# Column halves in two PSUM banks, four block places per parity, one output store: a masked prefix sum with a product, on one core

## The chip, the core and the metric

The kernel runs on one core of one Trainium2 chip. The metric is the device time of one execution in microseconds (us). Each figure is the median of several executions. A "span" is one execution as the hardware profiler recorded it; it is some 2 us shorter than the timed figure of the same execution (86.72 beside 88.84). An execution is called slow when it lies over 1.5% above the fastest of the same kernel; fast is compared with fast.

## The reference

```python
B, S, D = 8, 8192, 512
mask = pos < lengths                      # lengths: 8 numbers between 16 and 8191
cs = np.cumsum(x * mask, axis=1)          # x: [8, 8192, 512] float32
mid_features = cs[b, lengths[b] // 2]     # one row of 512 numbers per batch row
out = mid_features @ w                    # w: [512, 512]; out: [8, 512]
```

Only one element of the prefix sum is used, so a batch row needs the plain sum of its first n = min(length, length // 2 + 1) positions. For this draw n is 570, 2690, 256, 2057, 905, 3772, 3859 and 571. Nothing else of x is read: 31.2 MB with the weights.

## The kernel before

A batch row is cut into whole blocks of 512 positions (a `[128, 4, 512]` tile, 1 MB) and a remainder below 512. The first block of row 0 has a buffer of its own. That leaves 1, 5, 0, 4, 1, 7, 7 and 1 whole blocks for rows 0 to 7. SyncE (SP) issues the blocks, ScalarE (ACT) the remainders, TensorE adds everything up in one PSUM bank: the weights are a 128 x 8 selector with ones in the row's column, and the four position groups j of a block go to four column groups of the array (`tile_position`), so four matmuls run side by side (in the trace the eight records of a block, 0.77 us each in the mean, fit into 1.04 to 1.90 us). Rows of even and odd number ("parity" q) have separate buffers.

```python
NB = S // 2 // BLK                                   # 8
xt = sb("xt", [P, 2, NB, G, D])                      # 8 places per parity
s_ps = ps("s_ps", [P, D])                            # one bank, 512 columns
...
# SyncE, for each row; base, n from the lengths
def load_block(k):
    take(sp, s_free[q][k], 1)                        # wait for the place, count down
    sp.dma_start(out=xt[:, q, k], in_=...).then_inc(s_full[q][k], 16)
...
# TensorE, for each row: remainder first, then its blocks
take(pe, s_rem[q], 16 * (len(PARTS) + 1))
for j in range(G):
    mm = add(j, cur[:, q, B + j * B:2 * B + j * B], rem[:, q, j])
mm.then_inc(s_rfree[q], 1)
def add_block(k):
    take(pe, s_full[q][k], 16)
    for j in range(G):
        mm = add(j, cur[:, q, :B], xt[:, q, k, j])   # 128x512 each
    mm.then_inc(s_free[q][k], 1)                     # the place is free again
whole_blocks(pe, ns.rows(q), add_block)
...
# the end: VectorE copies sums (two halves), TensorE folds, VectorE copies,
# TensorE multiplies by wt, then
for j in range(2):   # VectorE; ScalarE does j = 2, 3 into o_sb[1]
    step(dve.tensor_copy, out=o_sb[0][:, j * P:(j + 1) * P], in_=o_ps[32 * j:32 * j + B, :P])
sp.dma_start(out=out[:, :D // 2], in_=o_sb[0][:]).then_inc(s_out, 16)
act.dma_start(out=out[:, D // 2:], in_=o_sb[1][:]).then_inc(s_out, 16)
```

The row loop is a hardware loop over pairs of rows; the block count of a row is known only from the lengths, in registers (`whole_blocks` nests comparisons). Each row starts again at place 0.

## Time and profile before

| | before |
|---|---|
| timed, median (4 fast runs) | 88.96 us (88.77 to 89.65) |
| profiled span | 86.72 us |
| first block issued by SP | 5.07 us |
| last block of x landed | 79.08 us |
| from there to the end of the span | 7.64 us |
| TensorE busy | 49.5 us (57%) |
| transfers, mean over the span | 361 GB/s (some 420 while they run) |

The table reads as three stretches: a start of some 4 us until data flow, a middle in which the transfer engines set the pace, and a tail in series after the last landing.

### The profile page before, as it was taken

To read this page: it belongs to the slowest core of one execution; us is meant where nothing else is said; L and a number is where in the kernel's file an instruction comes from. 1 tells how busy PE (TensorE), PEld (TensorE's weight loads), DVE (VectorE), ACT (ScalarE), POOL (GpSimd) and SP (SyncE) were. 2 spreads that over 40 slices of the span, in tenths; PEclk is the share of its full clock that TensorE was granted. 3 is DMA by queue.
4 is the path that set the end of the run, shared out by engine and by line. 5 is a ranking of instruction groups with operands and counts; after the bars stand their busy time and mean duration, and the time that the engine had idled before them with its cause. 6 is when DMAs were issued, how large, how long until landed. Compare 5 with 4: busy or idle time off the path is not lost. (4 is left out here: it accounts for less than half of the span.)

```text
span 86.7 us, 1276 instructions
## 1 busy us (share of the span) xinstructions
PE 49.5 (57%) x317; PEld 9.1 (10%) x317; DVE 8.1 (9%) x42; ACT 2.0 (2%) x4; POOL 4.0 (5%) x9
## 2 busy tenths in 40 slices
PE   0910533999367627179833268877933348779720
PEld 0400000022011000012100000001100000011710
DVE  3685000000000000000000000000000000000520
ACT  0000000000000000000005100000000000000020
POOL 0980000000000000000000000000000000000000
PEclk9999999999999996557998555555999985559995
DMA  2799999999999999999999999999999999980000
GB/s 30 325 412 283 397 417 420 430 427 419 419 408 416 416 423 423 401 416 423 423 423 419 416 428 423 423 423 408 423 423 423 423 419 419 423 359 15 0 4 3
DMA packets 4693, 31.28 MB, mean 361 GB/s; under 512 B 658, under 2 KB 674, under 8 KB 946
## 3 DMA queue, kind: packets, MB, share of 16 engines
q1 hardware_dynamic: 3762, 27.27, 76.5%
q10 hardware_dynamic: 928, 3.97, 11.7%
q8 instruction: 1, 0.02, 0.1%
q14 instruction: 2, 0.02, 0.0%
HBM read 31.23 MB, written 0.02 MB: 360 GB/s over the span
## 5 line engine op out<-in xcount | busy, mean ns | idle before, releaser
L339 PE MATMUL s_ps<-xt,cur 128*8 128x512 f32 x200 | 34.0, 771 | 21.9 <-PEq L103 21.8
L339 PE MATMUL s_ps<-rem,cur 128*8 128x512 f32 x64 | 10.5, 738 | 3.6 <-PEq L103 3.6
L339 PEld LDWEIGHTS s_ps<-xt,cur 128*8 128x8 f32 x200 | 4.3, 91 | 50.5 <-issue 50.4
L322 DVE COPY cur<-table 128x40 f32<-128x40 f32 x8 | 1.4, 184 | 53.0 <-PE s_ps L339 53.0
L339 PE MATMUL s_ps<-first,first_w 128*8 128x512 f32 x8 | 1.9, 1040 | 5.1 <-DMA first<-in_x_dram 5.1
L257 POOL MEMSET rem<- 128x2048 f32 x2 | 3.5, 1804 | 0.0
L347 PE MATMUL s_ps<-zero 1*128 1x512 f32 x2 | 2.1, 1131 | 2.4 <-DVE n_i L268 2.4
L339 PEld LDWEIGHTS s_ps<-rem,cur 128*8 128x8 f32 x64 | 1.6, 93 | 13.1 <-issue 13.0
L268 DVE COPY s_sb<-s_ps 128x256 f32<-128x256 f32 x2 | 0.8, 425 | 18.4 <-PE s_ps L376 18.4
L240 ACT ACT_TABLE_LOAD x1 | 1.3, 1283 | 46.5 <-issue 46.5
L382 PE MATMUL mf_ps<-fold,s_sb 128*128 128x8 f32 x8 | 1.1, 260 | 0.5 <-DVE s_sb L268 0.5
L243 ACT COPY o_sb<-o_ps 8x128 f32<-8x128 f32 x2 | 0.5, 260 | 35.0 <-PE o_ps L390 35.0
L390 PE MATMUL o_ps<-wt,mf_sb 128*8 128x128 f32 x32 | 1.1, 273 | 0.0
L382 PEld LDWEIGHTS mf_ps<-fold,s_sb 128*128 128x128 f32 x8 | 1.0, 190 | 0.6 <-DVE s_sb L268 0.6
L350 PEld LDWEIGHTS n_ps<-n_f,ones 1*128 1x128 f32 x2 | 0.7, 332 | 1.0 <-DVE table L268 0.5
L390 PEld LDWEIGHTS o_ps<-wt,mf_sb 128*8 128x8 f32 x32 | 0.8, 89 | 0.0
L347 PEld LDWEIGHTS s_ps<-zero 1*128 1x128 f32 x2 | 0.5, 304 | 2.3 <-DVE n_i L268 2.3
L339 PEld LDWEIGHTS s_ps<-first,first_w 128*8 128x8 f32 x8 | 0.2, 90 | 5.1 <-issue 5.1
L268 DVE COPY o_sb<-o_ps 8x128 f32<-8x128 f32 x2 | 0.6, 280 | 0.9 <-PE o_ps L390 0.8
L268 DVE MEMSET zero<- 1x512 f32 x1 | 0.5, 485 | 1.1 <-SPq L48 1.1
L268 DVE TENSOR_SCALAR thr_i<-thr_i 128x2 int32<-128x2 int32 x1 | 0.5, 484 | 0.0
L350 PE MATMUL n_ps<-n_f,ones 1*128 1x8 f32 x2 | 0.4, 286 | 0.0
(36 smaller groups left out, 5.5 us busy)
## 6 DMA issues: line engine op xcount, KB each, us to landing
xt<-in_x_dram SPq DMA_DIRECT2D x25, 1024.0 KB, 14.4
rem<-in_x_dram ACTq DMA_DIRECT2D x3, 512.0 KB, 7.1
wt<-in_w_dram ACTq DMA_DIRECT2D x1, 1024.0 KB, 6.8
first<-in_x_dram SPq DMA_DIRECT2D x1, 1024.0 KB, 8.2
rem<-in_x_dram ACTq DMA_DIRECT2D x3, 256.0 KB, 6.5
rem<-in_x_dram ACTq DMA_DIRECT2D x3, 128.0 KB, 6.6
rem<-in_x_dram ACTq DMA_DIRECT2D x3, 32.0 KB, 5.8
rem<-in_x_dram ACTq DMA_DIRECT2D x1, 64.0 KB, 6.1
```

Of the source, the lines that this page charges most:

```text
L240: act.copy(out=warm[:], in_=zero[:, :1])
L243: copy = act.copy(out=o_sb[1][:, j * P:(j + 1) * P], in_=o_ps[64 + 32 * j:64 + 32 * j + B, :P])
L257: pool.memset(rem[:, q], 0.0).then_inc(s_rfree[q], 1)
L268: do(*args, **kw).then_inc(s_dve, 1)
L322: dve.tensor_copy(out=cur[:, b % 2], in_=table[:, b * WT:(b + 1) * WT]).then_inc(s_cur[b % 2], 1)
L339: return pe.matmul(s_ps[32 * j:32 * j + B], lhsT=weights, rhs=rows, start=False, stop=False, skip_group_check=True, tile_position=(0, 32 * j))
L347: pe.matmul(s_ps[:], lhsT=zero[:, :P], rhs=zero[:], start=True, stop=False, skip_group_check=True)
L350: pe.matmul(n_ps[:, :B], lhsT=ones[:], rhs=n_f[:], start=True, stop=True).then_inc(s_pe, 1)
L382: mm = pe.matmul(mf_ps[h][:, i * B:(i + 1) * B], lhsT=s_sb[:, 2 * h + i], rhs=fold[:], start=True, stop=True)
L390: mm = pe.matmul(o_ps[32 * j:32 * j + B, :P], lhsT=mf_sb[:, kc], rhs=wt[:, kc, j * P:(j + 1) * P], start=(kc == 0), stop=(kc == KC - 1), t ...
```

## The change

The intent: let the first half of the columns finish early, so that its copy and its fold lie beside the second half's matmuls (two PSUM banks, a chained counter `s_half`); let all four output quarters be one copy and one store; let SyncE load only the lengths of two rows at a time, so that it issues its first block earlier; and halve the buffers of the blocks: eight places of 1 MB per parity become four.

```diff
+    NP = 4
-    xt = sb("xt", [P, 2, NB, G, D])
+    xt = sb("xt", [P, 2, NP, G, D])
-    s_ps = ps("s_ps", [P, D])
+    s_ps = [ps(f"s_ps{h}", [P, D]) for h in range(2)]
-    mf_sb = sb("mf_sb", [P, KC, B])
-    o_sb = [sb(f"o_sb{h}", [B, D // 2]) for h in range(2)]
+    mf_sb = sb("mf_sb", [P, KC, 32])
+    o_sb = sb("o_sb", [P, P])
-    ctx.enter_context(tc.tile_critical(no_gpsimd_drain=True))
+    ctx.enter_context(tc.tile_critical(sync_engine=mybir.EngineType.Pool, no_gpsimd_drain=True))
@@ SyncE
-        ns = Counts(sp, s_len1, 16)
+        ns = Counts(sp, s_len1, 16, loaded=2)     # next_pair() loads the next 4 words
-                    take(sp, s_free[q][k], 1)
-                    sp.dma_start(out=xt[:, q, k], ...).then_inc(s_full[q][k], 16)
+                    take(sp, s_free[q][k % NP], 1)
+                    sp.dma_start(out=xt[:, q, k % NP], ...).then_inc(s_full[q][k % NP], 16)
-        sp.dma_start(out=out[:, :D // 2], in_=o_sb[0][:]).then_inc(s_out, 16)
+        sp.dma_start(out=out.rearrange("b (j c) -> j b c", c=P), in_=o_sb[::4]).then_inc(s_out, 16)
@@ ScalarE: its two copies, its activation table and its store are gone
@@ VectorE
+        dve.wait_ge(s_half, due)                  # due: blocks + remainders, from the lengths
         for h in range(2):
+            if h:
+                dve.wait_ge(s_pe, B + 2)
-            step(dve.tensor_copy, out=s_sb[:, 2 * h:2 * h + 2], in_=cols[:, 2 * h:2 * h + 2])
+            step(dve.tensor_copy, out=s_sb[:, 2 * h:2 * h + 2], in_=s_ps[h][:, :H]...)
-        for j in range(2):
-            step(dve.tensor_copy, out=o_sb[0][:, ...], in_=o_ps[32 * j:32 * j + B, :P])
+        step(dve.tensor_copy, out=o_sb[:], in_=o_ps[:, :P])
@@ TensorE
+            for h in range(2):
+                for j in range(G):
+                    mm = pe.matmul(s_ps[h][32 * j:32 * j + B, :H], lhsT=weights[j],
+                                   rhs=rows[:, j, h * H:(h + 1) * H], ...)
+                mm.then_inc((half, done)[h], 1)
-                        whole_blocks(pe, ns.rows(q), add_block)
+                    with pe.Fori(0, NB // NP):
+                        whole_blocks(pe, n, NP, add_block)
+                        pe.reg_alu(n, n, NP * BLK, ALU.subtract)
+                        pe.reg_alu(n, n, 0, ALU.max)
```

Cut: the matching changes of counts and semaphores, the column order of the weights, and the split of TensorE's program into two branches (`sums()`, `product()`).

## The prediction

> **What bounds the kernel now.** I read the page's slices first, then the groups of instructions, the DMA issues, the waits of the load queue, and last the chain and the end of the timeline. In the slices the transfers run full from slice 2 to slice 35 of 40, and nothing else does:
>
> ```profile
> PE   0910533999367627179833268877933348779720
> DMA  2799999999999999999999999999999999980000
> GB/s 30 325 412 283 397 417 420 430 427 419 419 408 416 416 423 423 401 416 423 423 423 419 416 428 423 423 423 408 423 423 423 423 419 419 423 359 15 0 4 3
> ```
>
> A slice is 86.7/40 = 2.17 us. From about 4 us to 78 us the 16 transfer engines move some 420 GB/s; the one hole is slice 3 (283). So the middle costs bytes over rate: a block of 128 x 4 x 512 floats is 1.05 MB, 2.49 us. TensorE only follows:
>
> ```profile
> L339 PE MATMUL s_ps<-xt,cur 128*8 128x512 f32 x200 | 34.0, 771 | 21.9 <-PEq L103 21.8
> ```
>
> It stood idle 21.9 us ahead of the block sums, nearly all of it in line 103, the taking of a "full" semaphore. A cheaper TensorE, fewer matmuls or fewer waits there buy nothing in the middle; what can move the time is (a) a hole in the transfers, and (b) what comes before the first and after the last transfer. The end, in the timeline:
>
> ```profile
> 79.21 1.04 PE L339 MATMUL s_ps<-xt,cur 128*8 128x512 f32 x8
> 80.19 0.17 PE L376 MATMUL s_ps<-zb 1*32 1x1 bf16 x1
> 80.40 0.88 DVE L268 COPY s_sb<-s_ps 128x256 f32<-128x256 f32 x2 [18.36 <-PE s_ps L376]
> 80.88 1.07 PE L382 MATMUL mf_ps<-fold,s_sb 128*128 128x8 f32 x8 [0.52 <-DVE s_sb L268]
> 81.88 1.06 PE L390 MATMUL o_ps<-wt,mf_sb 128*8 128x128 f32 x32
> 83.00 0.59 DVE L268 COPY o_sb<-o_ps 8x128 f32<-8x128 f32 x2 [0.84 <-PE o_ps L390]
> 83.56 0.58 ACTq L246 DMA_DIRECT2D out_dram<-o_sb  x1
> 83.63 0.36 SPq L191 DMA_DIRECT2D out_dram<-o_sb  x1
> ```
>
> The last block lands at 79.1; then 7.6 us in series: sums, copy, fold, copy, product, copy, store, closing handshake. How far ahead the loads are issued is in the issues and in the load queue's own waits:
>
> ```profile
> xt<-in_x_dram SPq DMA_DIRECT2D x25, 1024.0 KB, 14.4
> ...
> SPq L103 <- SPq L103: 21.6, 8, 9.2
> ```
>
> A block lands 14.4 us (median) after its issue, so about six blocks' worth of bytes (14.4/2.49) stand queued. The queue's own 21.6 us of waiting for free places does no harm only because of that depth.
>
> **What the Trainium skill says.** (1) "PSUM — Partial Sum Buffer", Terms: TensorE writing and VectorE reading the same bank and quadrant at once is an error. So a copy of half the sums beside the other half's matmuls needs two banks, as the change has. The trace agrees in so far as the copy begins only after the closing matmul (80.19, then 80.40). (2) "DMA: Bandwidth & Descriptors", Anatomy of one DMA: a fixed cost of about 2.0 us per transfer besides its bytes (stated for the GpSimd path). This trace, on the hardware queues: the weights' transfer was issued at 0.92, and the stretch 0 to 2.8 us moved 47 GB/s on average, the next 0.4 us 328; so data come about 2 us after the issue on an idle queue. (3) Same page, "Why a DMA increments its semaphore by 16 and not by 1": the engine count is the largest up to 16 that divides both sides' slowest dimension. The new store has slowest dimensions 32 and 4, so by that it would use 4 engines; no run yet shows it. (4) "TensorE: Matmul & The Clock Gate", Part 1: the clock is at half or full, set by recent activity. The trace has both: a block's eight matmul records take 1.04 us at full clock and 1.89 at half.
>
> **The change part by part.**
>
> Four places instead of eight per parity. The lengths of this draw give rows of 570, 2690, 256, 2057, 905, 3772, 3859 and 571 summed positions, so whole blocks 1, 5, 0, 4, 1, 7, 7, 1 (the first one of row 0 has its own buffer). Rows 1, 3, 5, 7 share parity 1. Block k of a row goes to place k modulo 4, and each row begins at place 0 again. Before, row 1 fills places 0 to 4, and row 3's block 0 waits for row 1's block 0. After, row 1's block 4 goes to place 0, and row 3's block 0 needs that same place: it can be issued only when row 1's *last* block is summed. Row 2 has no block. So at that moment no block is in flight at all, and SP issues in order, so nothing behind it can go out either. This is the step that I expect to decide.
>
> Size of that hole. Before, row 1's block 4 was issued at 8.87 and landed 15.6 later, at 24.5. After, its issue waits for row 1's block 0, summed at about 20.0 (SP's next issue, into that place, is at 20.24). Its data then come from 22 on; row 2's remainder (512 KB, issued 16.89) fills most of that gap, so it lands at about 24.4 still. Then: 0.15 to the first matmul, 1.04 for the sums, 0.05 for the semaphore (25.65); 0.22 for SP to take it and issue (20.01 to 20.24 in this trace); 2.0 until data: 27.9. A packet of 8 KB takes 0.31 at full flow, so flow is back at 27.6. The transfer engines ran dry not at 24.4 but spread over the 1.2 us before (first to last engine's landing of one block), on average 23.8. Loss 27.6 - 23.8 = **3.8 us**. Only the 32 KB remainder of row 3 can fill it: row 4's is issued after row 2's remainder is summed (27.19 now). Since every later byte queues behind, the whole loss goes to the end.
>
> Other places where four bind: rows 5 and 6 (7 blocks). Block 4 of a row waits for its block 0, with blocks 1 to 3 in flight: 3 x 2.49 = 7.5 us against some 4.0 for sum, issue and latency (1.9 + 0.2 + 2.0, half clock). Row 7's block 0 needs a place that row 5 freed long ago. No hole: 0.
>
> Two banks, sums by column halves. A block is 16 records of 256 columns in place of 8 of 512: the same columns. I take the same 0.86 to 1.04 us (1.9 at half clock), under 2.49 in any case: 0 in the middle. At the end half 0 is done about 0.43 earlier, so its copy (0.43) and its fold lie beside the matmuls of half 1. Before: copy, copy, fold, fold with the second copy and half the folds in the chain. The chain loses about one copy, 0.43; but TensorE's sequencer must leave two nested loops and a second branch before the closing matmul and the fold, which I put at 0.2. Gain **0.25**.
>
> Output: one copy of 128 x 128 for two of 8 x 128 (0.28 each, the partitions don't count): gain **0.3**. One store on SP alone instead of two; if 4 engines carry 8 pieces of 512 B each, the landing is some 0.2 later: **-0.2**. GpSimd leads the closing handshake rather than SP: after the landing SP no longer starts a round and collects it: **0.25**, an estimate from the 1.5 us between landing (85.1) and end.
>
> Lengths by pairs. SP loads 4 register words instead of 16 before its first block issue at 5.07. If half of the load's 1.2 us goes with the words, it is 0.4 earlier. That shrinks the hole at 8 us:
>
> ```profile
> 8.00:9.00 1.00, 0.00 (x0) 0.00 (x0) 0.00 (x0) 0.00 (x0) 0.00 (x0) 1.00 0.58 197
> 9.00:10.00 1.00, 0.30 (x4) 0.15 (x8) 0.00 (x0) 0.00 (x0) 0.00 (x0) 1.00 1.07 426
> ```
>
> There 0.5 us of flow is missing ((426-197)/426), and 0.2 in the us before (344). I take **0.25** of it. The later loads of pairs (four of about 0.8) lie in SP's waits: 0. The dropped activation table load (1.28 at 46.5) and the smaller clearing matmuls are beside transfers: 0.
>
> Sum: +3.8 - 0.25 - 0.3 + 0.2 - 0.25 - 0.25 = **+2.95**; I take off 0.3, because the hole might be partly filled by remainders. 88.94 + 2.65 = **91.6 us**.
>
> **The rivals.** (A) The hole isn't there or is small, because enough is queued. For it: four blocks are 10 us of transfers, and in the rows of seven this suffices. Against it: the place arithmetic above, where the last block itself holds the place. If it held, only gains of 0.85 remain: 88.1. (B) TensorE becomes the bound: 16 short matmuls with 16 weight loads (91 ns each) and two increments per block. For it: at half clock a block already takes 1.89 of 2.49. Against it: the matmuls work on four column groups side by side and the weight loads overlap. If the cost rose by a third at half clock, some 20 blocks would go to 2.5: at most +1 more. (C) The last block falls in a half-clock phase: 1.89 for 1.04 and slower products, +1.0 at the end; in the trace before it fell in a full-clock one (1.00 there). (D) The hole is wider: the sum of row 1's block 4 at half clock, +0.85, or the loop's second pass and instruction fetch on TensorE, +0.5.
>
> **Range and chances.** The hole, 3.3 to 4.5; gains, 0.4 to 1.6; C adds up to 1. That is 90.2 to 92.9 for 8 in 10. Two per cent slower is 90.72, so slower 0.75; within 2% 0.20 (a hole under 2.7, or gains at their upper end with it); faster, under 87.16, needs A and larger gains: 0.05.
>
> **What would show it.** In the slices of after: one slice near 24 to 28 us falls from 420 to under 150 GB/s, and its neighbour dips; all later slices at 420; last landing near 82. SP's longest waits for a place include one that ends just after row 1's last block is summed, and the next block's issue stands at about 25.9, not 20.2. The end from last landing to end of span takes about 7.0 us for 7.6; the first copy of sums starts before the last block's matmuls end. First block issue near 4.6. The prediction is wrong if the slices from 22 to 30 us stay at 420, if a second hole appears in rows 5 to 7, or if blocks' matmuls exceed 2.4 us.

## The result

The changed kernel took 94.31 us (median of 4 runs: 93.89, 94.09, 94.52 and 95.42, the last one slow) against 88.96. The ratio is 1.0571, 95% interval 1.0487 to 1.0654: **slower by 5.7%**, some 5.3 us. The predicted direction was right, but 91.6 and the range to 92.9 were too low. (A ratio here is the mean time of one kernel's fast runs over the mean of the other's fast runs of the same rounds, so it is not quite the ratio of the medians that I quote.)

The profiled spans differ by 5.96 us, 86.72 and 92.68. The clock of TensorE, the share and the flow of the transfers in 40 slices of 2.32 us, after:

```profile
PEclk9999999999985985555579975555589998556998
DMA  2899999966708999999999999999999999970000
GB/s 28 332 426 426 415 412 414 417 262 187 294 0 301 428 424 420 419 420 424 424 424 424 408 422 419 428 417 424 424 424 424 421 424 417 417 308 0 0 9 2
```

Slice 3 (from 7 us) is full now, where the kernel before had its dip of 283. In its place there are **two** holes: slices 8 to 10 (18.5 to 25.5 us: 262, 187, 294) and slices 11 and 12 (0 and 301). From slice 13 on the flow is as before. What the queue of the block loads and TensorE waited for, after, in that order as three views (the issue group with its median time from issue to landing; the queue's waits: us in total, times, longest; TensorE's group for block sums: busy us, mean ns of one, idle us before it and what ended most of that):

```profile
xt<-in_x_dram SPq DMA_DIRECT2D x25, 1024.0 KB, 10.8
```

```profile
SPq L109 <- SPq L109: 46.5, 12, 12.8
```

```profile
L367 PE MATMUL s_ps<-xt,cur 128*8 128x256 f32 x400 | 35.7, 495 | 22.9 <-PEq L109 22.9
```

A block is in flight 10.8 us instead of 14.4, SP waits 46.5 us for free places instead of 21.6, and TensorE's busy time on blocks grew only from 34.0 to 35.7 us. So nothing on TensorE became a bound; the loads are issued later.

The holes by the microsecond. Columns: stretch, its length, busy time of PE, PEld, DVE and POOL, granted clock, DMA share, GB/s:

```profile
20.00:21.00 1.00, 1.00 (x24) 0.49 (x20) 0.00 (x0) 0.00 (x0) 1.00 0.18 74
21.00:22.00 1.00, 1.00 (x24) 0.46 (x20) 0.00 (x0) 0.00 (x0) 1.00 0.61 107
22.00:23.00 1.00, 0.84 (x16) 0.21 (x8) 0.00 (x0) 0.00 (x0) 1.00 0.58 238
...
25.00:26.00 1.00, 0.50 (x12) 0.33 (x16) 0.00 (x0) 0.00 (x0) 1.00 0.01 4
26.00:27.00 1.00, 0.74 (x16) 0.20 (x12) 0.00 (x0) 0.00 (x0) 1.00 0.00 0
27.00:28.00 1.00, 1.00 (x16) 0.36 (x8) 0.18 (x1) 0.00 (x0) 0.52 0.19 33
28.00:29.00 1.00, 0.95 (x15) 0.18 (x11) 0.00 (x0) 0.00 (x0) 0.50 0.54 180
29.00:30.00 1.00, 1.00 (x16) 0.30 (x8) 0.18 (x1) 0.00 (x0) 0.50 1.03 434
```

The same view of the kernel before (with a column for ACT ahead of POOL) is full in both places:

```profile
20.00:21.00 1.00, 1.00 (x12) 0.21 (x8) 0.00 (x0) 0.00 (x0) 0.00 (x0) 1.00 1.06 442
...
27.00:28.00 1.00, 0.82 (x8) 0.27 (x12) 0.00 (x0) 0.00 (x0) 0.00 (x0) 1.00 1.04 434
```

The end, from the timeline of after (start, length in us, engine, what it does, how many; in brackets the idle time before it and what ended it):

```profile
82.89 1.94 PE L367 MATMUL s_ps<-rem,cur 128*8 128x256 f32 x16
84.59 1.27 PE L367 MATMUL s_ps<-xt,cur 128*8 128x256 f32 x16
85.51 0.95 DVE L281 COPY s_sb<-s_ps 128x256 f32<-128x256 f32 x2 [18.73 <-PE s_ps L367]
85.80 0.17 PE L405 MATMUL s_ps<-zb 1*32 1x1 bf16 x1
85.99 1.14 PE L412 MATMUL mf_ps<-fold,s_sb 128*128 128x8 f32 x8
87.06 1.08 PE L420 MATMUL o_ps<-wt,mf_sb 128*32 128x128 f32 x32
88.21 0.29 DVE L281 COPY o_sb<-o_ps 128x128 f32<-128x128 f32 x1 [0.86 <-PE o_ps L420]
88.52 0.73 SPq L211 DMA_DIRECT2D out_dram<-o_sb  x1
```

The mechanism that the change aims at is there: the first copy of sums begins at 85.51, before the last sums end (85.86), and the output copy is one of 0.29. But the last sums end 2.3 us after the last landing (83.57), and the store lands at 91.35, 2.83 us after its issue.

The stages of the profiled executions side by side, read from the traces (us; each stage begins where the one above it ends). "After, again" is a second profile of the unaltered changed kernel, taken with other runs; "five places" and "pairs" are experiments told below.

| | before | after | after, again | five places | pairs |
|---|---|---|---|---|---|
| first block issued at | 5.07 | 4.33 | 4.33 | 4.33 | 4.38 |
| row 1's fifth block issued / landed | 8.87 / 24.45 | 20.56 / 25.37 | 19.94 / 24.98 | 7.81 / 25.26 | - / 24.27 |
| row 3's first block issued / landed | 20.24 / 27.14 | 26.84 / 31.60 | 26.45 / 31.42 | 20.52 / 27.81 | 19.88 / 26.91 |
| last block landed at | 79.08 | 83.57 | 83.33 | 79.68 | 78.85 |
| then: its sums end | 1.18 | 2.30 | 1.18 | 1.19 | 1.18 |
| closing matmul ends | 0.10 | 0.10 | 0.70 | 0.70 | 0.10 |
| fold and product end | 2.58 | 2.17 | 3.00 | 2.14 | 2.58 |
| store issued | 0.63 | 0.39 | 0.39 | 0.39 | 0.63 |
| store landed | 1.57 | 2.83 | 2.59 | 2.62 | 1.57 |
| end of the span | 1.58 | 1.32 | 1.32 | 1.35 | 1.57 |
| span | 86.72 | 92.68 | 92.52 | 88.06 | 86.48 |

So of the 5.96 us, 4.49 stand at the last landing and 1.47 in the tail. I had put +3.25 (3.8 - 0.25 - 0.3) and -0.6 there. Both are off, the tail by more.

### The profile page after: what moved, and what is told of

It is laid out like the page before. It is cut to its first block, busy times and chain, and to the rows that moved or that the text cites. A ratio compares the mean times of both kernels' runs of the same rounds, so it can differ in the third digit from the quotient of the medians.

```text
span 92.7 us, 1874 instructions
## 1 busy us (share of the span) xinstructions
PE 53.0 (57%) x589; PEld 18.8 (20%) x589; DVE 10.1 (11%) x40; POOL 4.0 (4%) x9
## 5 line engine op out<-in xcount | busy, mean ns | idle before, releaser
L367 PE MATMUL s_ps<-xt,cur 128*8 128x256 f32 x400 | 35.7, 495 | 22.9 <-PEq L109 22.9
L367 PEld LDWEIGHTS s_ps<-xt,cur 128*8 128x8 f32 x400 | 11.6, 104 | 46.4 <-issue 43.2
L367 PE MATMUL s_ps<-rem,cur 128*8 128x256 f32 x128 | 14.3, 590 | 2.8 <-PEq L109 2.6
L367 PEld LDWEIGHTS s_ps<-rem,cur 128*8 128x8 f32 x128 | 4.2, 115 | 12.0 <-issue 11.6
L377 PE MATMUL s_ps<-zb 1*128 1x256 bf16 x2 | 0.6, 399 | 7.6 <-DVE sh L281 7.6
L367 PE MATMUL s_ps<-first,first_w 128*8 128x256 f32 x16 | 1.9, 624 | 1.9 <-DVE table L281 1.9
L281 DVE TENSOR_SCALAR n_i<-n_i 1x8 int32<-1x8 int32 x1 | 1.7, 1733 | 0.0
L281 DVE TENSOR_SCALAR n_i<-lens 1x8 int32<-1x8 int32 x1 | 1.6, 1628 | 0.7 <-DMA lens<-in_lengths_dram 0.7
L420 PE MATMUL o_ps<-wt,mf_sb 128*32 128x128 f32 x32 | 1.1, 276 | 0.0
L420 PEld LDWEIGHTS o_ps<-wt,mf_sb 128*32 128x32 f32 x32 | 0.8, 109 | 0.0
## 6 DMA issues: line engine op xcount, KB each, us to landing
xt<-in_x_dram SPq DMA_DIRECT2D x25, 1024.0 KB, 10.8
```

Of the source, the lines that this page charges most:

```text
L281: do(*args, **kw).then_inc(s_dve, 1)
L367: mm = pe.matmul(s_ps[h][32 * j:32 * j + B, :H], lhsT=weights[j], rhs=rows[:, j, h * H:(h + 1) * H], start=False, stop=False, skip_group_c ...
L377: pe.matmul(s_ps[h][:, :H], lhsT=zb[:, :P], rhs=zb[:], start=True, stop=False, skip_group_check=True)
L420: mm = pe.matmul(o_ps[32 * j:32 * j + 32, :P], lhsT=mf_sb[:, kc], rhs=wt[:, kc, j * P:(j + 1) * P], start=(kc == 0), stop=(kc == KC - 1), ...
```

## The experiments

Twelve runs were made, of eleven kernels (after_again repeats the changed kernel, a_np5_oldout2 repeats a_np5_oldout). Those of one group ran on the same chip in turn with the kernel before: a_np8, a_np5, b_np4 and a_store4 (before: 89.55); after_again, b_pairs, a_np5_oldout and a_blocksfirst (89.0); b_pairs_pool and a_np5_oldout2 (89.59); a_np5_adj4 and b_np4_turn each alone. All gave a correct result.

| label | what it is | median us | ratio to before, 95% |
|---|---|---|---|
| after_again | the changed kernel once more | 94.43 | 1.0557 [1.0426, 1.0688] |
| b_np4 | before, four places | 94.76 | 1.0666 [1.0559, 1.0773] |
| a_np5 | after, five places | 90.39 | 1.0144 [1.0062, 1.0226] |
| a_np8 | after, eight places | 92.30 | 1.0326 [1.0247, 1.0405] |
| b_np4_turn | before, four places in another order | 95.74 | 1.0645 [1.0448, 1.0843] |
| a_blocksfirst | after, a row's blocks before its remainder | 96.38 | 1.0702 [1.0563, 1.0841] |
| a_store4 | after, four stores | 94.76 | 1.0590 [1.0496, 1.0684] |
| a_np5_oldout | five places, output part of before | 89.15 | 0.9950 [0.9825, 1.0074] |
| a_np5_oldout2 | the same kernel | 89.26 | 0.9979 [0.9920, 1.0038] |
| a_np5_adj4 | five places, four stores of adjacent partitions | 90.41 (before 90.23), one run each | - | unknown |
| b_pairs | before, lengths by pairs | 89.50 | 1.0046 [0.9950, 1.0143] |
| b_pairs_pool | b_pairs, closing handshake led by GpSimd | 89.01 | 0.9964 [0.9902, 1.0025] |

At a threshold of 2%, after_again, b_np4, a_np8, a_blocksfirst and a_store4 are slower than before; a_np5 and b_np4_turn (only two fast runs: 94.15 and 95.52) are unclear; both runs of a_np5_oldout, b_pairs and b_pairs_pool are the same.

My theory was that the place arithmetic makes the holes. Its rivals: the smaller buffer as such (fewer bytes queued), TensorE's sixteen matmuls and its instruction fetches, and the tail.

**Four places alone, and one place more.** b_np4 is the kernel before with

```diff
+    NP = 4
-    xt = sb("xt", [P, 2, NB, G, D])
+    xt = sb("xt", [P, 2, NP, G, D])
-    take(sp, s_free[q][k], 1)            # and likewise in every use of a place
+    take(sp, s_free[q][k % NP], 1)
```

> The kernel before with four places per parity (block k in place k modulo 4) and nothing else of the change. Theory 1: both holes appear; the first smaller than in the changed kernel (about 1.4 for 2.1 us, since SP starts later by 0.7), the second 3.7; last landing 83.3 to 84.0, time 92.8 to 94.3. Rival (other parts of the change made the holes): 89 to 90.

a_np5 is the changed kernel with

```diff
-    NP = 4
+    NP = 5
-                    with pe.Fori(0, NB // NP):
+                    with pe.Fori(0, -(-NB // NP)):
```

> The changed kernel with five places per parity; nothing else. Theory 1 (place arithmetic: row 1 has five blocks, so none of its places is used twice): same as with eight places, within 1%, last landing 78.3 to 79.5, no hole between 19 and 29 us. Rival (depth: simply too few bytes queued, 4 MB a parity): five give only a quarter more, so a good part of the holes stays, time over 91.5.

The flow in 40 slices of b_np4:

```profile
GB/s 32 341 412 355 437 405 434 430 292 82 313 92 75 419 434 419 419 430 412 423 423 416 437 411 418 412 437 416 427 416 416 430 416 430 419 427 156 0 0 7
```

and of a_np5:

```profile
GB/s 35 301 422 424 412 387 427 419 413 421 380 417 421 417 409 420 424 417 417 421 417 420 415 431 421 424 417 421 417 417 421 428 428 424 417 112 0 0 10 1
```

The places alone bring both holes into the kernel before (292, 82, 313 and 92, 75) and a slowdown as large as that of the whole change: 1.0666. But it is made up differently: all of it stands at the last landing, none in the tail (7.50 us for 7.64). It is also more than I expected: the first hole lost 3.1 us and not 1.4, and the last landing (84.69) and the time lie above what I had named. (In that profile the lengths happened to land 1.0 us later than in the one of before, 3.18 against 2.16, so its first issue is at 6.07; its last landing holds part of that.) One place more takes both holes out of the changed kernel. Summed over 18 to 31 us, the flow missing against 424 GB/s was worth 5.9 us in after (2.18 up to 24.2 us, then 3.73), 0.33 in a_np5, 6.8 in b_np4 and 0.19 in before. Five places are 1 MB more per parity, and well below the eight of before; so what counts is hardly the amount queued. The next experiment holds the amount fixed. The timed ratio falls from 1.0571 to 1.0144: going from five places to four makes some 3.9 us of the change's 5.3 (the last landing moves from 79.68 to 83.57, the median from 90.39 to 94.31).

**Another order of the same four places.** b_np4_turn keeps b_np4's 4 MB per parity and only turns the order:

```diff
+    PL = [0, 1, 2, 3, 1, 2, 3, 0]
-    take(sp, s_free[q][k % NP], 1)       # and likewise in every use of a place
+    take(sp, s_free[q][PL[k]], 1)
```

> The kernel before with four places per parity, but the places of a row's blocks are taken in the order 0, 1, 2, 3, 1, 2, 3, 0 in place of 0, 1, 2, 3, 0, 1, 2, 3: the same 4 MB per parity, only row 1's fifth block now goes to place 1, and row 3's first block still to place 0. Theory of the place clash: row 3's block 0 no longer needs the place of row 1's last block, so it is issued right behind it (at about 23 us, where four places in the plain order had 28.00) and lands before 30.5 (32.74); row 1's fifth block waits for one more block's sums, so it is issued 0.9 to 1.0 later than the 21.86 there and the first hole grows by about that; row 3's block 1 now needs the place of row 1's fifth block, which makes a smaller hole of 1 to 1.5 us. Together some 1.5 us less lost than in the plain order: last landing about 83.2 (84.69), time 93.0 to 93.8 (94.76). Rival, that the amount buffered and not the order of the places decides: row 3's block 0 is issued no earlier than 27 and the time stays at 94.5 or more.

```profile
GB/s 28 332 433 255 375 414 433 415 377 168 408 363 91 408 433 429 422 410 428 422 415 433 401 426 429 408 415 419 422 426 380 377 401 321 363 227 10 0 0 7
```

In the middle it did what the clash theory asks: row 3's first block was issued at 23.44 instead of 28.00 and landed at 29.37 instead of 32.74 (some of b_np4's lateness is that of its lengths: its fifth block went out 0.66 later, at 21.86 for 21.20), a smaller hole of the next block followed (slice 12), and the flow missing from 18 to 34 us was 4.0 us instead of 6.8. But the time did not follow: 95.74 where I expected 93.0 to 93.8, and the two fast runs are no faster than b_np4's. In the profile (a slow execution, so I take only the order of events from it) the slices from 30 on are thin (380, 377, 401, 321, 363, 227): 358 GB/s over 72 to 80 us where b_np4 had 422, and the last block landed at 85.40. In this order row 6's fifth block waits for its *second* block's sums, with two blocks in flight behind it instead of three. That this is why the flow thinned there is argued, not shown. What it settles is that the order decides when row 3's first block can go out, and so the second hole; it does not make four places usable.

**Eight places in the changed kernel.**

```diff
-    NP = 4
+    NP = 8
```

> The changed kernel with eight places per parity again (the inner loop then runs once); all other parts stay. Theory 1 (a place needed by a row's last block, taken again by row 3's first, and row 1's fifth block waiting for its first): both holes between 19 and 29 us vanish, the transfers stay near 420 GB/s, the last landing is back at 78.3 to 79.1, and the time 88.0 to 90.0. Rival (sums by halves, longer code or the loop nest on TensorE hold the loads back): holes remain and the time stays over 92.

I meant it as the plain control, and it is not one: 1.0326, with a hole where the places cannot make one.

```profile
GB/s 29 300 419 431 414 412 413 413 385 367 90 126 417 428 417 428 410 419 426 413 435 417 416 417 421 428 417 417 431 417 420 431 413 420 431 255 7 0 17 1
```

Two lines of its timeline tell why: row 0's remainder begins in TensorE at 16.95, and the next remainder's weight load only at 21.32, after 3.36 us in which TensorE waited for nothing that the profile shows.

```profile
16.95 1.94 PE L367 MATMUL s_ps<-rem,cur 128*8 128x256 f32 x16
...
21.32 0.15 PEld L367 LDWEIGHTS s_ps<-rem,cur 128*8 128x8 f32 x8 [3.36 <-issue]
```

In the trace TensorE's sequencer stood in one branch from 16.44 for 4.33 us, and two instruction fetches of 16 KB began in it, at 16.5 and 16.6, and took 1.9 and 2.1 us (a third, at 22.5, took 1.1). Row 3's first block, which waits for the sums of row 1's first one, went out at 25.10 instead of 20.24. With eight places TensorE's nested program is twice as deep; that this makes the fetches fits, but no run changed it alone. So five places, not eight, are the control.

**A row's blocks before its remainder.** If the first hole comes from row 1's fifth block waiting for its first block's sums, which wait for the remainders, then summing blocks first should shrink it. In `sums()` the taking and adding of the remainder goes below the blocks:

```diff
-                    take(pe, s_rem[q], 16 * (len(PARTS) + 1))
-                    add(... rem[:, q] ...)
                     with pe.Fori(0, NB // NP):
                         whole_blocks(pe, n, NP, add_block)
                         ...
+                    take(pe, s_rem[q], 16 * (len(PARTS) + 1))
+                    add(... rem[:, q] ...)
```

> The changed kernel (four places) with a row's whole blocks summed ahead of its remainder. Row 1's block 0 is then summed some 1.9 us earlier, so its fifth block is issued at about 18.5 rather than 20.6. Theory of two separate holes: the first shrinks from 2.1 to under 0.8 us, the second (row 3's block 0 waiting for row 1's last) stays 3.5 to 3.9; last landing 1.3 to 2 earlier than in the changed kernel, while the last remainder's sums come after the last block and cost 0.9 to 1.9 at the end: 93 to 95. Rival (one hole, set by the number of places alone): the loss of flow stays at 5.5 to 6.

```profile
GB/s 14 362 438 417 399 433 403 427 293 293 31 28 372 421 421 431 407 424 414 431 424 404 434 417 421 414 434 421 414 427 407 431 424 414 417 3 0 0 9 2
```

A miss. In the profile (a slow execution, so again only the order of events counts) the block was issued 1.9 us earlier (18.70), but landed at 25.54, later than before: the first of the 16 transfer engines had its part down at 22.92, the last one 2.6 us later. The holes lost 6.25 us together. So the first hole's size is not simply issue plus a fixed delay, and I could not settle why the parts of that block spread over 2.6 us.

**The changed kernel once more.**

> The changed kernel unaltered, for a second profile and times on the chip of this group. If the 2.3 us from last landing to the end of the sums were a chance of the half-clock phase: about 1.2 now, with the same holes (slices between 19 and 29 us) and last landing 83.4 to 84.3. If they belong to the kernel (halves make TensorE slower): again over 2. Time 93.8 to 95.

It reproduced the time (1.0557), the holes (1.95 and 3.90 us) and the slow store (2.59). It did not reproduce the late last sums: the clock of TensorE fell to half elsewhere. The last sums ended 1.18 us after the landing, the closing matmul came late, and the product ran at half clock, 1.94 us for 1.08:

```profile
83.47 1.05 PE L367 MATMUL s_ps<-xt,cur 128*8 128x256 f32 x16 [0.55 <-PEq L109]
...
85.05 0.16 PE L405 MATMUL s_ps<-zb 1*32 1x1 bf16 x1 [0.54 <-issue]
...
86.28 1.94 PE L420 MATMUL o_ps<-wt,mf_sb 128*32 128x128 f32 x32
```

**The output store.** a_store4 replaces the one store of 32 partitions by four of 8 partitions, on two queues:

```diff
-        sp.dma_start(out=out.rearrange("b (j c) -> j b c", c=P), in_=o_sb[::4]).then_inc(s_out, 16)
+        for j in (0, 2):     # j = 1, 3 the same on ScalarE's queue; final wait 64
+            sp.dma_start(out=out[:, j * P:(j + 1) * P], in_=o_sb[32 * j:32 * j + 32:4]).then_inc(s_out, 16)
```

> The changed kernel with the one store of 32 pieces cut into four stores of 8 partitions (two on SP, two on ACT), so that each may use 8 engines. Theory 3 (the one store is slow for its 4 engines with 8 pieces each, 2.8 us from issue to landing for 1.5 before): 1.6 to 2.0 us from the first issue to the last landing, time 93.2 to 93.7. Rival (the 2.8 us were an instruction fetch that happened to hold one engine): unchanged in the mean, 94.0 to 94.6, with the holes as before in both.

It landed 3.31 us after its first issue, later than the one store. This doesn't clear the four engines: the four issues took so long, one after the other on each queue, that the last went out 1.55 us after the first, and it landed 1.76 us later. The rival named in its text, a fetch that holds one engine, comes back below. a_np5_oldout gives the five-place kernel the output part of before: mf_sb without padding, two copies of 8 x 128 on each of VectorE and ScalarE, two stores of 8 adjacent partitions.

> The five-place version of the changed kernel with the output part of the kernel before: rows of the product not spread, two copies on DVE and two on ACT, two stores of 8 adjacent partitions. Theory (the one store costs 2.6 to 2.8 us from issue to landing because of how it is formed, partitions in steps of 4): 1.5 to 1.6 here, copies 0.3 longer, so 0.7 to 0.9 faster than five places with one store (90.4 to about 89.6 where before is 89.5). Rival (the store is slow because of the new handshake or an instruction fetch at its side): 2.4 or more again, so 0.3 slower.

> The five-place version with the old output part, again, beside the one above: the two differ by the sums in two banks with the loop nest, and by the number of places. If the chain of halves gains what was predicted (0.25 us), it is the faster of the two; if the later closing matmul (0.6) eats the gain of 0.43 and the loads' slowest engine is later by 0.4, it is 0.3 to 0.8 slower than that one (ratio to before 0.998 to 1.006).

("The one above" in the second text is b_pairs_pool, told below; 0.998 and its 0.996 do not tell the two apart.) The store landed 1.83 us after its issue (1.98 in the second run, whose profile is slow), and the ratio fell from 1.0144 to 0.995 and 0.998. So the new output part costs some 1.6 to 1.9% by itself; from the intervals of a_np5 and of the second run I estimate 0.7 to 2.6%. a_np5_adj4 is to be compared with a_store4: one 128 x 128 copy and four stores again, but of 8 adjacent partitions each (`o_sb[32 * j:32 * j + B]`). Beside that it has five places and the unpadded mf_sb.

> Five places, one copy of the product, and four stores of 8 adjacent partitions with 512 B each (two on SP, two on ACT). Beside the earlier four stores of 8 partitions in steps of 4 it changes the partition step alone. If the step makes the store slow: 0.3 to 0.4 us per issue on SP and some 0.85 from the issue to its first bytes, as in the kernel before. If the 512 B pieces do (1024 B before): 0.65 to 0.8 per issue and 1.3 to 1.4 to the first bytes again.

Its issues in the timeline; SP's 0.73 here are two, 0.36 and 0.31:

```profile
84.36 0.73 SPq L212 DMA_DIRECT2D out_dram<-o_sb  x2
```

and the one of a_np5_oldout:

```profile
84.30 0.36 SPq L213 DMA_DIRECT2D out_dram<-o_sb  x1
```

An issue of adjacent partitions costs SP 0.31 to 0.36 us; with a step of four partitions an issue cost 0.65 to 0.81. First bytes move 0.8 us after the issue, against 1.3 to 1.4. Still a_np5_adj4's stores landed only 2.82 us after the first issue (a single run, its state unknown; its last store was issued 0.61 us after the first).

The traces show what the step does not explain. In every form of the changed kernel an instruction fetch of 8 KB (0.37 to 0.63 us) begins some 1.2 us after the store's issue; in before the one at the end comes only 4.96 us after it. In the five traces with the one store (after, after_again, a_np5, a_np8, a_blocksfirst) three of its four engines had landed 1.90 to 1.94 us after the issue, some 0.36 us later than all of before's store. The eight pieces of the fourth began to move when the fetch ended (1.69 to 1.89 us after the issue, the same in each trace to 0.02), and it landed at 2.59 to 2.83. With before's form of store (a_np5_oldout) all pieces had moved when the fetch began, and the landing was 0.26 and 0.41 us later than in before. So of the 1.0 to 1.3 us that the one store costs, some 0.36 are in all its engines, and 0.66 to 0.90 are in the one engine whose pieces wait for the fetch. The trace doesn't number the engines, so that the fetch runs on this one is inferred from the times; I had no kernel in which it alone was moved.

**Lengths by pairs, and the handshake.** b_pairs is the kernel before with the new `Counts` and `next_pair`:

```diff
-        ns = Counts(sp, s_len1, 16)
+        ns = Counts(sp, s_len1, 16, loaded=2)
```

> The kernel before with SP loading the lengths by pairs, nothing else. Theory: the first block is issued 0.7 us earlier, the hole at 8 us closes, and as no later hole swallows it the last landing comes 0.5 to 0.8 earlier: 0.5 to 0.8 us faster than before. Rival (one transfer engine lags anyway and sets every landing): last landing unchanged, within 0.2 us.

Columns as for the kernel before:

```profile
7.00:8.00 1.00, 0.00 (x0) 0.00 (x0) 0.84 (x5) 0.00 (x0) 0.00 (x0) 1.00 0.96 401
8.00:9.00 1.00, 0.00 (x0) 0.00 (x0) 0.00 (x0) 0.00 (x0) 0.00 (x0) 1.00 0.99 418
```

The first issue came 0.69 us earlier and the hole at 8 us is gone (418 for 197), yet the last landing moved only from 79.08 to 78.85 and the time not at all. The parts of the last block landed over 1.68 us instead of 1.14 (first to last of the 16 transfer engines): a block is as late as its latest engine. One engine is late from the beginning in every kernel, by 2.26 us after the first already at the weights in before. Behind a hole the parts land close together again (0.33 us at the last block of after, 2.28 in a_np5). If a hole lets late engines catch up, closing it gives back less than its width; that this is why b_pairs gained so little is argued.

b_pairs_pool adds the other closing handshake, `sync_engine=mybir.EngineType.Pool`:

> The kernel before with the two parts of the change that measured as gains by themselves: lengths by pairs on SP and GpSimd leading the closing handshake. From the profiles: last landing 0.2 earlier, end of span 0.25 earlier after the landing of the output: 0.3 to 0.6 us faster than before (ratio 0.993 to 0.997). Rival (noise covers it, or the handshake's gain belongs to the single store): ratio 0.998 to 1.003, and 1.5 us from landing to end as before.

From store landed to end of span: 1.44 us, for 1.57 without. The time is the same as before within its interval. No version that I ran is clearly faster than the kernel before.

## Why the prediction was right or wrong

**Right: the mechanism and its place.** The working said that row 3's first block needs the place of row 1's last one, and can go out only when that is summed. b_np4 makes the holes alone, a_np5 takes them away, b_np4_turn moves the issue by 4.6 us (0.66 us of that because the fifth block, too, went out earlier). Between row 1's fifth block's landing and row 3's issue lay 1.47 us (25.37 to 26.84, and again 1.47 in the second profile); the sum of terms gave 1.46. Rival A (no hole) is false; so is rival B (TensorE as bound): a block at full clock took 1.04 to 1.05 us in both kernels and 1.89 to 1.90 at half. And so is rival D: row 1's last block was summed in 1.05 us, at full clock, and the issue followed as reckoned.

**Failed: "row 2's remainder ... fills most of that gap, so it lands at about 24.4 still."** This is the step in "Size of that hole" that failed. The first hole was taken as filled. The remainder had passed at 19 to 20.5 us; in 20 to 22 there was nothing left to move (74 and 107 GB/s). The first hole missed 2.18 us of flow, and the fifth block landed at 25.37, 0.97 late (24.98 in the second profile, 0.58 late).

**Mis-sized: "flow is back at 27.6".** From the landing on, the steps added up as reckoned until the issue; then data took longer to come. Row 3's block landed at 31.60, where the sum gave 27.6 + 2.49 = 30.1; 0.97 of the 1.5 us is the first hole's, 0.54 the return of the flow: only 180 GB/s in 28 to 29 us (in the second profile 0.58 and 0.74). I had read one delay of 2.0 us out of averages over long stretches. The packets show two: in before the weights' first ones began at 2.00, 1.1 us after the issue, and here row 3's at 27.82, 1.0 after it; the full rate came only near 29.

**Mis-sized: pairs, 0.25, and the safety, 0.3.** The first issue came 0.74 earlier and the hole at 8 us closed, as said. But the fifth block's issue waits for the sums of row 1's first block, about 20.2 us, which wait for remainders that land at 16.4; in after nothing of the early issue reaches past that (in its second profile they land at 15.82 and the fifth block goes out at 19.94). And without other holes, b_pairs' last landing gained 0.23, near the 0.25, while its time did not show it. The 0.3 us that I took off for remainders filling the hole had no ground: nothing filled it. Together: last landing +4.49 and +4.25 in two profiles, for +3.25.

**Mis-sized in the tail: the store, -0.2.** I had it landing 0.2 us later; it landed 1.26 and 1.02 us later. The four engines were right (the trace ends the store in four semaphore writes) but not the cost. I had counted bytes and pieces, and neither the issue and the reading of every fourth partition, nor the fetch that one engine's pieces waited for.

**Wrong sign: the chain, +0.25 as a gain.** At full clock the fold and product chain gained 0.44 (2.58 to 2.14 in a_np5), as the halves were meant to; but the closing matmul came 0.60 late, where I had put 0.2 for leaving the loops. Net loss about 0.16. In a_np8, whose inner loop runs once and not twice, the closing matmul ended 0.10 us after the sums as in before, so it seems to be the second pass that costs this.

**Right: copies and handshake.** Product end to store issue fell by 0.24 (predicted 0.3), landing to end by 0.26 (0.25).

**Rival C came true in both profiles of after**, in two forms: last sums at half clock (+1.1), or product at half clock (+0.86). It didn't in a_np5, a_store4 and a_np8, and a_np5_oldout had it; so had b_np4_turn, which has nothing else of the change (its last sums ended 2.17 us after the landing). The matmuls are no costlier, so I call it a matter of where the clock's phases fall when the end is shifted; that is argued from these few profiles. I had named +1.0 for it and given it room in the range only beside larger gains.

In all: the tail is +1.47 and +1.54 instead of -0.6, the last landing +4.5 and +4.25 instead of +3.25. The span grew by 5.96 us where my sum had 2.65. Of the 3.3 us between, 1.24 stand at the last landing (the first hole and the slower return of the flow), 1.06 are the store and 1.12 the last sums at half clock; the other terms together came out 0.1 better than put. So the direction was no luck, since the second hole is there as argued; the size failed on those three. The five-place kernel checks the sum: landing +0.60 and tail +0.74 make 1.34 us of span, and its ratio of 1.0144 is 1.3 us.

Open: why single transfer engines lag, and by how much that stretches a given hole (a_blocksfirst); why b_np4_turn lost its gain near the end; whether the instruction fetch alone holds back the store's fourth engine.

## What to carry to other kernels

When you shrink a ring of buffers, don't ask only whether enough bytes stay queued: write down which place each load takes and which work frees it, for the real sequence of lengths, and look for a load that needs the place of the load just ahead of it. One place more or fewer can decide it. A hole's size is best reckoned from when the bytes queued ahead of it really pass, and an output store's cost from its issue, its partition step and what else the transfer engines carry just then, not from its bytes.

## What the Trainium skill lacked or had wrong

- "DMA: Bandwidth & Descriptors", Why a DMA increments its semaphore by 16 and not by 1: the rule for the engine count agrees (four engines for the new store, four semaphore writes in the trace). What no page gives is the cost of a partition step on the SBUF side: with a step of four SP's issue took 0.65 to 0.81 us and first bytes came 1.3 to 1.4 us after it; with adjacent partitions 0.31 to 0.36 and 0.8.
- "Runtime: NRT & Kernel Launch", Instruction fetch mechanics: it says that a taken branch out of the two-page window stalls until the page is fetched. The runs fit it (two fetches began in a_np8's stall at 16.44) and give the size that the page lacks: branches of 4.3 to 5.7 us in a_np8, and one of 5.26 us in after (at 1.64, hidden at the start). The page also lacks how long a fetch lasts: one of 16 KB took 0.9 to 1.1 us here, up to 2.1, and one of 8 KB at the end 0.37 to 0.63, with eight pieces of the store starting just as it ended. That fetches delay blocks of x on the same engine is argued, not shown.
- The same section gives some 200 ns per register for a register load, stated for loads from HBM. Here, from SBUF, 16 words took 1.19 us and 4 words 0.50 at first and 0.30 to 0.31 later: (1.19 - 0.50) / 12 is about 0.06 us per further word.
